# Pre-summed quarters of w2 made by accumulating transfers, the sampled tokens' output product placed inside an MLP product, a norm shift on another engine

## Chip, cores and metric

One core of a Trainium2 chip runs the whole program. The metric is the device time in microseconds from launch to end. The kernel before took 3325.08 us as the median of three runs (3316.52 to 3332.91). Everything is float32 on the outside. On TensorE each float32 product is made of three passes over a high and a low part of the operands, which are split by ScalarE (high part) and VectorE (low part).

## The reference, cut to what matters

One layer of a decoder: a joint input projection, a causal attention with forget gates (FoX) and a matrix memory (mLSTM) over 2048 prompt tokens, the same for 64 sampled tokens against a paged cache of 8192 positions per sequence, an output projection, and an MLP, with a layer norm after each.

```python
def _block_out(x, fox_h, m_h, og, mlstm_norm_w, w_o, ln1_g, ln1_b, w1, w2, ln2_g, ln2_b):
    ...
    mix = jnp.concatenate([fox_h, mn.astype(x.dtype)], axis=-1) @ w_o
    x1 = _layer_norm(DN_ALPHA * x + mix, ln1_g, ln1_b)
    hid = jnp.square(jax.nn.relu(x1 @ w1))
    return _layer_norm(DN_ALPHA * x1 + hid @ w2, ln2_g, ln2_b)
```

## The kernel before

The work runs in four stages on one core. Stage A (up to about 920 us) projects the inputs and runs the matrix memory. Stage B is the prompt's attention: 64 units, one for each head `h` (0 to 7) and group `g` (0 to 7) of 256 queries. Stage O multiplies the mixed heads by `w_o` and makes the first layer norm. Stage C is the MLP in four blocks of 512 tokens (`ci` 0 to 3); the fourth block also holds the 64 sampled tokens, as tile 16.

**The attention of the sampled tokens** is a generator of 294 steps that runs beside all of this. `tick(us)` adds modelled microseconds of TensorE work to a counter and takes one step of the generator for each `PACE` of them; `PACE_C` holds in stages O and C. A step of even number multiplies one gathered pair of cache pages; step `n` handles pair `(n - 38) / 2`, so the last of 128 pairs falls to step 292. Step 293 ends the last sequence, and then the result is written to DRAM (`dmix`). Seventy-eight steps and the gathers behind them are done when stage O begins. A call of `unit` in stage O is worth 5.1 modelled microseconds, a half of `hidden` 5.12, each of the 14 half products of `output` 1.28.

**The MLP** of a block goes over 16 slices of 256 hidden columns. `hidden(p, half)` makes one slice `hq` from `w1`, in two halves `f` = 0, 1 of 128 columns, and `output(p)` multiplies two slices by `w2` in seven products instead of eight (a Strassen-like scheme over 2 by 2 quarters). Four of the seven need sums of quarters of `w2`: b11+b12, b12+b22, b22+b11+b12 and b21+b22+b11+b12. They do not depend on the tokens, so they are made once, in stage B, by `w2_sums(p)` for `p` = 0 to 7, and kept in DRAM as `dw2`. One call loads the four quarters (512 KB each) through SyncE's queue into `wr` buffers, of which there are five, adds them in place on GpSimd in a chain of four additions (L1089), and stores each sum through GpSimd's queue (L1090). It is called at every sixth unit from unit 8 to unit 50.

**In stage B**, GpSimd also adds the causal mask to a row of forget values for each 128 queries (`nd`, L938, three buffers). VectorE's masked maximum of the diagonal block (L956) needs `nd`, and everything behind it on VectorE waits for it. VectorE also makes the low parts of queries and keys (`ql`, `ks`, L157, two SBUF inputs), and TensorE's scores (L945, L946) wait for these. ScalarE makes the exponentials (L973).

**The sampled tokens' end.** When the attention of the sampled tokens is through, `sampled()` reads `dmix` for them, multiplies it by `w_o` (eight pieces of weights, each split by ScalarE and VectorE), makes the first layer norm and stores it to `dx1`. The fourth block's last tile is read from there and transposed by TensorE (`px`, L1135) before that block can begin. In the third block (`ci` = 2) this is traced after `output(6)`, then `hidden(7, 1)`, then the rest of the attention's steps, then `sampled()`, then `output(7)`, which also transposes the next block's tiles.

**Second layer norms** of blocks 0 to 2 are carried out one by one in the next block's `hidden` calls (`later`): statistics on VectorE, power on GpSimd (L174), scale on ScalarE (L176), gain on VectorE (L177), shift on GpSimd (L178). The fourth block has a quicker form, `norm_quick`, which the change does not touch.

**The order of instructions** on an engine is chosen when the program is built: from the trace order, by a simulated timeline, so an instruction that is ready in that simulation can stand ahead of one traced earlier. `issue_after(ins)` keeps the instructions of its block behind `ins` on `ins`'s engine. At run time each engine takes its instructions in order.

Of the kernel before, what the change touches and what calls it, by code (L numbers as in the profile page):

```python
# [19 lines left out]

PACE_A = 5.6
PACE_B = float('inf')
PACE_C = 5
PACE_M = 2.3
D = 1024
S = 2048
# [26 lines left out]
def body(ctx, tc, I, O, stages):  # L53
# [811 lines left out]
    def phase_b():  # L865
# [172 lines left out]
        for n in range(len(units) + LA):  # L1038
            if 10 <= n < 16 and acc[1] is not None:
                attend()  # L1040
            if n % 6 == 2 and 8 <= n < 56:
                w2_sums(n // 6 - 1)
            if n == 60:
                wo.extend(half_wo(0, q) for q in range(4))
            if n < len(units):
                h, g = units[n]
                sc[n] = scores(Z[h], g)
                if h == 0 and g % 2 == 0 and g < 6:
                    keys(Z[0], g // 2 + 1)
                if h < 7:  # L1050
                    if g == 3:
                        Z[h + 1] = head(h + 1)
                        forget_values(Z[h + 1], 0, S)
                    if g >= 4:
                        keys(Z[h + 1], g - 4)
                if n + 1 < len(units):
                    queries(Z[units[n + 1][0]], units[n + 1][1])
            if n >= LA:
                h, g = units[n - LA]
                values(Z[h], g, sc.pop(n - LA))  # L1060
# [19 lines left out]

        return pcw.tile([128, 1024], F32, name="xr", bufs=2)[:n]

    def w2_sums(p):

        b11, b12, b21, b22 = (raw() for _ in range(4))
        for q, b in enumerate((b11, b12, b21, b22)):
            SY.dma_start(b, I["w2"][p, q])
        for q, (a, b) in enumerate(((b11, b12), (b12, b22), (b22, b11), (b21, b22))):
            G.tensor_tensor(a, a, b, op=OP.add)  # L1089
            G.dma_start(dw2[p, q], a)  # L1090

    def half_wo(hf, q):

# [46 lines left out]
    def phase_o(halves):  # L1140
        C["py"] = es_c.enter_context(tc.tile_pool(name="py", bufs=1, side="right", reuse_waits="tile"))
        C["pc"] = pc = es_c.enter_context(tc.tile_pool(name="pc", bufs=1, reuse_waits="tile"))
        es, es_b, es_x = ExitStack(), ExitStack(), ExitStack()
        po_ = es.enter_context(tc.tile_pool(name="po", bufs=1, reuse_waits="tile"))
        pob = es_b.enter_context(tc.tile_pool(name="pob", bufs=1, side="right", reuse_waits="tile"))
        ppo = es.enter_context(tc.tile_pool(name="ppo", bufs=1, space=PSUM, reuse_waits="tile"))

        def mix(t, eng):
            mr = landing().rearrange("p (k c) -> p k c", k=8)
            SY.dma_start(mr, dmv[:, :, t * 128:(t + 1) * 128])  # L1150
            mh = po_.tile([128, 8, 128], F32R, name="mh", bufs=2)
            ml = po_.tile([128, 8, 128], F32R, name="ml", bufs=2)
            split_hi(mh, mr)
            split_lo(ml, mr, mh, eng)
            return mh, ml

        vx["more"] = lambda: pob.tile([128, 1024], F32, name="vx", bufs=2)
        wh, wl = [[], []], [[], []]

        def weights(hf):  # L1160
            for q in range(4):
                r = halves.pop(0) if halves else half_wo(hf, q)
                if hf == 0:
                    h, l = piece(None, r)
                else:
                    h = pob.tile([128, 2, 512], F32R, name="woh", bufs=4)
                    l = pob.tile([128, 2, 512], F32R, name="wol", bufs=4)
                    split_hi(h, r)
                    split_lo(l, r, h)
                wh[hf] += [h[:, 0], h[:, 1]]  # L1170
                wl[hf] += [l[:, 0], l[:, 1]]

        m, xs = {}, {}

        def begin(t):
            xs[t] = row()
            SY.dma_start(xs[t], x_of(t))

        def unit(t, hf):
            s = slice(hf * 512, (hf + 1) * 512)  # L1180
            ps = ppo.tile([128, 512], F32, name="pw", bufs=4)
            for k in range(8):
                mm3(ps, m[t][0][:, k], m[t][1][:, k], wh[hf][k], wl[hf][k], k == 0, k == 7)
            V.scalar_tensor_tensor(xs[t][:, s], xs[t][:, s], ALPHA, ps, op0=OP.mult, op1=OP.add)
            tick(5.1)

        def end(t):
            layer_norm(xs[t], 128, *gb, pc, "1")
            SY.dma_start(dx1[t * 128:(t + 1) * 128], xs[t])

        m[0] = mix(0, None)
        weights(0)
        pad(pc, 192)
        m[1] = mix(1, None)
        begin(0)
        begin(1)
        unit(0, 0)
        weights(1)
        unit(1, 0)
        gb = [bcast(I[f"ln1_{x}"], 0, D, f"{x}1", pcw, tag="wr", bufs=5) for x in "gb"]  # L1200
        unit(0, 1)
        m[2] = mix(2, G)
        end(0)
        unit(1, 1)
        end(1)
        for t in range(2, 14):
            if t == 13:
                vx["more"] = None
            m[t + 1] = mix(t + 1, G)
            begin(t)  # L1210
            unit(t, 0)
            unit(t, 1)
            end(t)

        m[15] = mix(15, G)
        begin(14)
        begin(15)
        nx = [x1_load(0), x1_load(1)]
        unit(14, 1)
        take_back()  # L1220
        unit(15, 1)
        es_b.close()
        C["px"] = es_c.enter_context(tc.tile_pool(name="px", bufs=1, side="right", reuse_waits="tile"))
        ppx = es_x.enter_context(tc.tile_pool(name="ppx", bufs=1, space=PSUM, side="right", reuse_waits="tile"))
        px_of = lambda: ppx.tile([128, 4, 128], F32, name="px", bufs=2)
        x1_turn(0, 0, nx[0], px_of)
        nx.append(x1_load(2))
        unit(14, 0)
        x1_turn(1, 1, nx[1], px_of)
        nx.append(x1_load(3))  # L1230
        end(14)
        unit(15, 0)
        x1_turn(2, 2, nx[2], px_of)
        x1_turn(3, 3, nx[3], px_of)
        C["w1"] = w1_pieces(0)
        end(15)
        es_x.close()
        es.close()


    def phase_c():
# [41 lines left out]
        for ci, blk in enumerate(CB):  # L1283
# [3 lines left out]
            pieces = [(0, 512)] if W == 512 else [(0, 288), (288, 576)]  # L1287

            def hidden(p, half, between=None):
                w1p = C.pop("w1", None) or w1_pieces(half * 8 + p)  # L1290
                hq = H[p, half] = ph.tile([128, 2, 576], F32, name="hq", bufs=3)
                for f in range(2):
                    for (a, b) in pieces:
                        ps = ppc.tile([128, 512], F32, name="ph", tag="ph", bufs=2)[:, :b - a]
                        for k in range(8):
                            wh, wl = (x[:, k % 4, f * 128:(f + 1) * 128] for x in w1p[k // 4])
                            mm3(ps, wh, wl, xh[:, k, a:b], xl[:, k, a:b], k == 0, k == 7)
                        A.activation(hq[:, f, a:b], ps, AF.Relu)
                        A.activation(hq[:, f, a:b], hq[:, f, a:b], AF.Square)
                        tick((b - a) * 0.01)  # L1300
                    if f == 0 and between:
                        between()
                    if later:
                        later.pop(0)()
# [120 lines left out]

            def normed(t, y, gb):
                def go():
                    layer_norm(y, 128, *gb, pc, "2")
                    SY.dma_start(y_out(t), y)
                return go  # L1430

# [9 lines left out]
            for p in range(8):  # L1441
                pre = []
                if p < 7:
                    hidden(p + 1, 0, lambda: pre.append(ahead(p, 1, 5)))
                else:
                    pre.append(ahead(p, 1))
                if p == 6:
                    vx["more"] = None
                output(p, pre[0], begun if p == 7 and ci < 3 else None)
                if p == 7 and ci < 3:  # L1450
                    vx["more"] = landing
                    C["w1"] = w1_pieces(0)
                    C["gb"] = vecs(2)
                    later = [normed(t, ys[t], C["gb"]) for t in blk]
                if p == 6 and ci < 3:
                    take_back()
                    begun = [x1_load(t) for t in CB[ci + 1][:2]]
                if p < 7:
                    hidden(p + 1, 1)
                if p == 6 and ci == 2:  # L1460
                    while acc[1] is not None:
                        tick(100.0)
                    sampled()
        es.close()

    wo = []
# [430 lines left out]
```

## Time and profile before

| | |
|---|---|
| median of three runs | 3325.08 us (3316.52 to 3332.91) |
| the profiled execution | 3329.77 us, span 3328.0 us |
| granted TensorE clock, mean | 0.975 |
| TensorE busy | 3161.2 us, 95% |
| VectorE, ScalarE, GpSimd busy | 64%, 45%, 30% |
| HBM | 220 GB/s over the span |

In the views of the profile, PE is TensorE, DVE VectorE, ACT ScalarE, POOL GpSimd, SP SyncE; SPq, ACTq and POOLq are the sequencers that issue transfers. A row of a group names the line of the kernel, engine and operation, what is written from what (`out<-in`), the shape and the count, then the busy time and the mean of one in ns, and after the second bar the idle time of the engine just ahead of these instructions with what ended it. A row of windows gives the busy time of each engine in a stretch with the number of its instructions, then the granted clock (1.00 is full), the share of time in which the transfer engines were busy, and GB/s.

### The profile page before, as it was taken

The page shows a single profiled execution, that of the slowest core. Times are in us where ns is not written, and L with a number is a line of the kernel's source. Part 1 is how long each engine was busy: PE and PEld are TensorE (multiplying, and loading weights), DVE is VectorE, ACT ScalarE, POOL GpSimd, SP SyncE. Part 2 cuts the span into 40 slices and gives each one's busy share as a digit, 9 for nine tenths or more (in the row PEclk, how much of TensorE's full clock was granted, in tenths as well). Part 3 has the DMA queues.
Part 4 walks back from the last instruction along what each step waited for, and adds up shares of the span by engine and source line. Part 5 has one row for each costly group of instructions (what it writes and reads, how often), then busy time and mean ns, then how long its engine had stood idle before and what let it go on. Part 6 is the DMA issues. An engine that isn't in the chain of part 4 may idle for free.

```text
span 3328.0 us, 58130 instructions
## 1 busy us (share of the span) xinstructions
PE 3161.2 (95%) x21681; PEld 2575.1 (77%) x21681; DVE 2128.3 (64%) x5067; ACT 1505.5 (45%) x2966; POOL 986.0 (30%) x989
## 2 busy tenths in 40 slices
PE   8999999988969999999899999999999999799997
PEld 8998998887846666677677777677777777698895
DVE  6957565455378887644465667666577666756658
ACT  4333343333357788622244444353454444444442
POOL 0031242322346622276433224323244211110000
PEclk9999999998989999999999999999999999899998
DMA  5575766756687732387788877878789666544333
GB/s 184 156 220 186 231 221 220 259 201 225 197 254 247 244 103 61 113 309 247 276 301 285 289 276 268 333 250 314 283 287 341 237 214 211 181 155 127 114 108 98
DMA packets 339698, 734.37 MB, mean 221 GB/s; under 512 B 63640, under 2 KB 177688, under 8 KB 338520
## 3 DMA queue, kind: packets, MB, share of 16 engines
q1 hardware_dynamic: 257464, 433.49, 40.9%
q0 software_dynamic: 78912, 287.34, 23.2%
q10 hardware_dynamic: 3040, 9.83, 0.8%
q8 instruction: 171, 2.80, 0.3%
q14 instruction: 111, 0.91, 0.1%
HBM read 660.93 MB, written 69.60 MB: 220 GB/s over the span
## 4 chain that ended last, share of the span: by engine, by line
PE 41%; DMA 5%; issue 4%; DVE 2%; POOL 1%; ACT 0%; DVEq 0%; POOLq 0%; SPq 0%; ACTq 0%
PE ph L162 7%; PE ph L163 7%; PE ph L164 7%; PE py L162 5%; PE py L164 5%; PE py L163 5%; DMA vt<-cache_v,idxV 3%; PE sO L1753 2%; PE sQ L1641 2%; DMA xr<-cache_v,idxV 1%; DVE wl L157 1%; PE sT L1710 1%; DVE y L1316 1%; PE pw L163 0%; PE pw L164 0%
## 5 line engine op out<-in xcount | busy, mean ns | idle before, releaser
L157 DVE TENSOR_TENSOR wl<-wr,wh 128x1024 fp32r<-128x1024 f32 x364 | 451.6, 1243 | 377.8 <-ACT wh L154 377.3
L154 ACT ACTIVATE wh<-wr 128x1024 fp32r<-128x1024 f32 x364 | 382.9, 1054 | 352.9 <-PE ph L163 159.2
L1618 POOL DMA_INDIRECT kT<-cache_k,idxK x256 | 269.8, 1054 | 634.6 <-PE sQ L1641 572.9
L162 PE MATMUL ph<-x1h,wh 128*128 128x512 f32 (+1 forms) x1280 | 456.7, 357 | 0.5 <-DVE x1l L157 0.5
L163 PE MATMUL ph<-x1l,wh 128*128 128x512 f32 (+1 forms) x1280 | 454.0, 355 | 0.0
L164 PE MATMUL ph<-x1h,wl 128*128 128x512 f32 (+1 forms) x1280 | 451.7, 354 | 0.0
L162 PE MATMUL py<-wh,hh 128*128 128x512 f32 x896 | 356.0, 399 | 1.7 <-ACT hh L154 0.8
L163 PE MATMUL py<-wl,hh 128*128 128x512 f32 x896 | 352.1, 393 | 0.5 <-DVE wl L157 0.5
L164 PE MATMUL py<-wh,hl 128*128 128x512 f32 x896 | 350.0, 392 | 1.6 <-DVE hl L157 1.6
L1316 DVE TENSOR_TENSOR y<-y,py 128x512 f32<-128x512 f32 x416 | 280.8, 681 | 75.1 <-PE py L164 71.0
L162 PE MATMUL pm<-xh,whi 128*128 128x256 f32 (+1 forms) x1024 | 301.4, 294 | 0.1
L163 PE MATMUL pm<-xl,whi 128*128 128x256 f32 (+1 forms) x1024 | 296.8, 290 | 0.0
L164 PE MATMUL pm<-xh,wlo 128*128 128x256 f32 (+1 forms) x1024 | 295.9, 289 | 0.0
L162 PEld LDWEIGHTS ph<-x1h,wh 128*128 128x128 f32 x1280 | 241.7, 189 | 40.2 <-issue 7.0
L163 PEld LDWEIGHTS ph<-x1l,wh 128*128 128x128 f32 x1280 | 241.7, 189 | 33.4 <-issue 2.9
L164 PEld LDWEIGHTS ph<-x1h,wl 128*128 128x128 f32 x1280 | 241.4, 189 | 33.5 <-issue 2.9
L1729 POOL DMA_INDIRECT vt<-cache_v,idxV x164 | 171.1, 1043 | 301.6 <-PE sO L1753 228.8
L162 PE MATMUL pm<-whi,xh 128*128 128x256 f32 (+2 forms) x816 | 238.7, 293 | 8.2 <-ACT whi L154 8.2
L163 PE MATMUL pm<-wlo,xh 128*128 128x256 f32 (+2 forms) x816 | 234.2, 287 | 0.6 <-DVE wlo L157 0.6
L164 PE MATMUL pm<-whi,xl 128*128 128x256 f32 (+2 forms) x816 | 233.8, 287 | 0.0
L973 ACT ACTIVATE S<-S,mx 128x512 f32<-128x512 f32 (+2 forms) x320 | 207.7, 652 | 37.3 <-DVE mx L959 34.7
L162 PEld LDWEIGHTS py<-wh,hh 128*128 128x128 f32 x896 | 168.1, 188 | 52.5 <-issue 10.4
(370 smaller groups left out, 6934.9 us busy)
## 6 DMA issues: line engine op xcount, KB each, us to landing
wr<-w SPq DMA_DIRECT2D x256, 512.0 KB
wr<-dw SPq DMA_DIRECT2D x128, 512.0 KB
wra<-w_in SPq DMA_DIRECT2D x104, 512.0 KB
Rb<-dR SPq DMA_DIRECT2D x128, 128.0 KB
dw<-wr POOLq DMA_DIRECT2D x32, 512.0 KB, 4.2
xn<-xp_t SPq DMA_DIRECT2D x16, 512.0 KB
kn<-k_prompt SPq DMA_DIRECT2D x64, 128.0 KB
qn<-dq SPq DMA_DIRECT2D x128, 64.0 KB
```

The lines of the kernel that those rows point to most:

```text
L154: last["ACT"] = A.activation(dst, src, AF.Copy, scale=scale)
L157: r = (eng or V).tensor_tensor(dst, src, hi.bitcast(F32), op=OP.subtract)
L162: T.matmul(ps, wh, xh, start=first, stop=False, skip_group_check=shared)
L163: T.matmul(ps, wh, xl, start=False, stop=False, skip_group_check=shared)
L164: last["PE"] = T.matmul(ps, wl, xh, start=False, stop=stop, skip_group_check=shared)
L973: last["ACT"] = A.activation(sp[:, :w], sp[:, :w], AF.Exp, bias=mx[:, 7:8], accum_out=lp[:, k:k + 1])
L1316: V.tensor_tensor(y, y, ps, op=op)
L1618: G.indirect_dma_start(out=piece(n), out_offset=None, in_=ck, in_offset=IO(ap=idxK[:, b, j // 2, j % 2:j % 2 + 1], axis=0))
L1641: r = T.matmul(pq[h4 * 32:h4 * 32 + 32, hg].rearrange("p (k c) -> p k c", k=2), z["qb"][:, hd], kv, start=(db == 0), stop=(db == 1), skip_ ...
L1710: T.transpose(p[:, f], z["U"][u][:, hg, f].rearrange("p k t -> p (k t)"), ident)
L1729: G.indirect_dma_start(out=vt.rearrange("p f c -> p (f c)"), out_offset=None, in_=cv, in_offset=IO(ap=idxV[:, b, (kt % 4) * 4 + kt // 4, f ...
L1753: after_ = T.matmul(po[r:r + 32], z["PT"][:, hg, 2 * f + g, pg].rearrange("p h q -> p (h q)"), vts[f][:, g, hg * 256:(hg + 1) * 256], star ...
```

## The change

Five edits. (1) `w2_sums` becomes `w2_sum`, called 34 times, at every one and a half units from unit 10 to unit 59. Two quarters (b11 and b22) are loaded for each `p`, through ScalarE's queue; the others are added to them by transfers that accumulate into SBUF, issued by GpSimd; the sums are stored by GpSimd as before. The 32 additions on GpSimd are gone. (2) In the third block the remaining attention steps come ahead of `hidden(7, 1)`, and `sampled` is traced between that product's two halves instead of after it; `PACE_C` goes from 5 to 4.93. (3) The shift of the second layer norm of blocks 0 to 2 goes from GpSimd to VectorE. (4) At the end of stage O, tile 2 is transposed before the norm of tile 14 and the first-half product of tile 15 instead of after them. (5) The low parts of `w1` are kept behind the split that was traced last on VectorE.

```diff
-PACE_C = 5
+PACE_C = 4.93
...
-            if n % 6 == 2 and 8 <= n < 56:
-                w2_sums(n // 6 - 1)
+            while len(w2_done) < 34 and n >= 10 + len(w2_done) * 3 // 2:
+                w2_sum()
...
-    def w2_sums(p):
-
-        b11, b12, b21, b22 = (raw() for _ in range(4))
-        for q, b in enumerate((b11, b12, b21, b22)):
-            SY.dma_start(b, I["w2"][p, q])
-        for q, (a, b) in enumerate(((b11, b12), (b12, b22), (b22, b11), (b21, b22))):
-            G.tensor_tensor(a, a, b, op=OP.add)
-            G.dma_start(dw2[p, q], a)
+    w2_done, w2_q = [], {}
+
+    def w2_sum():
+
+        k = len(w2_done)
+        w2_done.append(k)
+
+        def load(p):
+            for q in (0, 3):
+                w2_q[p, q] = raw()
+                with tc.issue_after(last["ACT"].ins):
+                    A.dma_start(w2_q[p, q], I["w2"][p, q])
+
+        def add(p, a, q):
+            G.dma_start(w2_q[p, a], I["w2"][p, q], accum_op=OP.add)
+
+        def store(p, a, j):
+            G.dma_start(dw2[p, j], w2_q[p, a])
+
+        p, j = divmod(k, 4)
+        if k == 0:
+            load(0)
+        if j == 0:
+            if p:
+                store(p - 1, 0, 2)
+                add(p - 1, 0, 2)
+            if p < 8:
+                add(p, 0, 1)
+        elif j == 1:
+            if p:
+                store(p - 1, 0, 3)
+            if p < 8:
+                store(p, 0, 0)
+                add(p, 3, 1)
+        elif j == 2:
+            store(p, 3, 1)
+            add(p, 0, 3)
+        elif p < 7:
+            load(p + 1)
...
         end(14)
         unit(15, 0)
-        x1_turn(2, 2, nx[2], px_of)
...
             def hidden(p, half, between=None):
-                w1p = C.pop("w1", None) or w1_pieces(half * 8 + p)
+                with tc.issue_after(last["DVE"].ins):
+                    w1p = C.pop("w1", None) or w1_pieces(half * 8 + p)
...
-                    layer_norm(y, 128, *gb, pc, "2")
+                    layer_norm(y, 128, *gb, pc, "2", V)
...
-                if p < 7:
-                    hidden(p + 1, 1)
                 if p == 6 and ci == 2:
                     while acc[1] is not None:
                         tick(100.0)
-                    sampled()
+                if p < 7:
+                    hidden(p + 1, 1, sampled if p == 6 and ci == 2 else None)
```

(The line that transposes tile 2 now stands ahead of `end(14)`.)

More of the change, by code (lines that the diff above doesn't have):

```diff
@@ L1230, in phase_o @@
         nx.append(x1_load(3))
+        x1_turn(2, 2, nx[2], px_of)
         end(14)
         unit(15, 0)
-        x1_turn(2, 2, nx[2], px_of)
         x1_turn(3, 3, nx[3], px_of)
```

## The prediction

> **What bounds the kernel now.** I read the page first (busy shares, then the slices of PE and of the granted clock), then the windows of stage B, then the groups and waits of the stretches that stood out.
>
> ```profile
> span 3328.0 us, 58130 instructions
> PE 3161.2 (95%) x21681; PEld 2575.1 (77%) x21681; DVE 2128.3 (64%) x5067; ACT 1505.5 (45%) x2966; POOL 986.0 (30%) x989
> PE   8999999988969999999899999999999999799997
> PEclk9999999998989999999999999999999999899998
> ```
>
> TensorE sets the time: it is busy 3161 of 3328 us, so no edit can bring more than the 167 us of idle time and what the clock loses beside it. The change touches three of the stretches where that time lies: the first part of stage B (slices 12 to 14), the turn from stage O to C (slice 20), and the end of the third MLP block (slices 34 and 35). In stage B the sums of w2 fall between 958 and 1157 us; the stretch behind them has the same work without them.
>
> ```profile
> 958.00:1157.00 199.00, 178.62 (x1145) 125.56 (x1146) 171.26 (x560) 148.28 (x417) 136.08 (x132) 0.92 0.75 245
> 1157.00:1346.00 189.00, 186.97 (x1290) 129.28 (x1287) 150.78 (x615) 161.49 (x458) 44.97 (x75) 1.00 0.29 87
> ```
>
> With the sums TensorE does 1145 matmuls in 199 us, without them 1290 in 189 us (6.83 a us), at which rate the 1145 take 168 us. So the sums cost about **31 us**: 20.4 us of idle TensorE and the rest in the clock (0.92) and in slower rows. What ends the idle time:
>
> ```profile
> L945 PE MATMUL pS<-ks,qh 128*128 128x512 f32 (+2 forms) x131 | 59.0, 452 | 14.0 <-DVE mx L956 8.5 <-DVE mx L952 4.6 <-DVE mx L959 0.7
> L946 PE MATMUL pS<-ks,ql 128*128 128x512 f32 (+2 forms) x132 | 51.1, 390 | 4.1 <-DVE ql L157 4.1
> ...
> L945 PE MATMUL pS<-ks,qh 128*128 128x512 f32 (+2 forms) x142 | 59.8, 424 | 0.6 <-DVE mx L959 0.2
> L946 PE MATMUL pS<-ks,ql 128*128 128x512 f32 (+2 forms) x142 | 51.5, 367 | 0.0
> ...
> L157 DVE TENSOR_TENSOR ql<-qn,qh 128x256 fp32r<-128x256 f32 x27 | 32.4, 1200 | 0.1
> L157 DVE TENSOR_TENSOR ks<-kn,ks 64x512 fp32r<-64x512 f32 x15 | 20.3, 1362 | 0.4
> ...
> L157 DVE TENSOR_TENSOR ql<-qn,qh 128x256 fp32r<-128x256 f32 x29 | 13.7, 474 | 1.3 <-ACT qh L154 1.3
> L157 DVE TENSOR_TENSOR ks<-kn,ks 64x512 fp32r<-64x512 f32 x12 | 8.1, 691 | 1.1 <-ACT ks L154 0.8
> ```
>
> (First pair of each kind: 958 to 1157; second pair: 1157 to 1346.) VectorE is late, and the rows that grew are those with two operands in SBUF: a `ql` takes 1200 ns instead of 474, a `ks` 1362 instead of 691. That is 27 x 0.73 + 15 x 0.67 = 30 us of VectorE, the size of the loss. TensorE's waits go over from 18.1 us to 0.6 us.
>
> **The change part by part. The sums.** What leaves GpSimd and what stays:
>
> ```profile
> L1089 POOL TENSOR_TENSOR wr<-wr 128x1024 f32<-128x1024 f32 x32 | 76.3, 2385 | 17.7 <-DMA wr<-w 13.0 <-issue 4.3
> ...
> L1090 POOL DMA_DIRECT2D dw<-wr x32: 538/568/606, 959.5 to 1157.1; - x32
> ...
> DMA to landing us min/median/max: 2.9/4.2/6.2
> ...
> L938 POOL TENSOR_TENSOR nd<-nl,dmask 128x128 f32<-128x128 f32 x59 | 29.4, 502 | 122.0 <-DVE mx L956 79.7 <-DVE ls L974 37.3 <-DVE mx L959 4.9
> ...
> L1378 ACTq DMA_DIRECT2D y<-dx x17: 326/411/912, 1656.1 to 2932.4; - x17
> kT<-cache_k,idxK POOLq DMA_INDIRECT x256, 9.0
> ...
> DMA to landing us min/median/max: 4.0/9.4/15.0
> ```
>
> (The last row is the landing of the gathers into `xr`, the slowest in this trace.) The 32 additions, 76.3 us, go. GpSimd then issues 32 stores and 32 accumulating transfers, 64 x 0.568 = 36 us over units 10 to 59, beside 24% of other work (44.97 of 189 us): it has room. ScalarE issues 16 loads, 16 x 0.41 = 6.6 us, at 85% busy (161.49 of 189): TensorE covers it, and without that cover it costs 6.6. SyncE loses 32 loads. The transfers thin out: 64 in 199 us become 80 in 50 units.
>
> What is new is the waiting on GpSimd. A unit lasts 6.75 us:
>
> ```profile
> 958.00:1157.00 199.00, 59.15 (x447) 28.53 (x449) 10.18 (x25) 9.07 (x25) 0.92 0.75 245
> 1157.00:1346.00 189.00, 68.01 (x524) 32.58 (x520) 11.03 (x27) 9.87 (x28) 1.00 0.29 87
> ```
>
> (Windows of the instructions on `po`: TensorE, weight loads, VectorE, ScalarE; ScalarE empties `po` once a unit, 28 times in the 189 us.) Four calls serve one `p`, so they have 6 units, 40.5 us. In them the first buffer goes through three additions in series and one store that an addition must await: 3 L + 4.2 us, where L is the landing of an accumulating transfer. Nothing here shows L. From below it is the plain store's 4.2 us, from above the 15.0 us of the slowest gather. It reads its target too, so I take twice the plain one, about 8 us, near the gathers' 9.0. Then 3 x 8 + 4.2 = 28 us fit into 40.5. Behind a waiting GpSimd stand `nd` and the scaling of finished heads; `nd` has three buffers, 1.5 units or 10 us ahead, and in the quiet stretch GpSimd already idles 79.7 us for VectorE to free one. A wait up to 10 us is hidden by that; beyond it VectorE's L956 is late, then the scores.
>
> The Trainium skill (Collectives: The Full Stack, "The bandwidth ceiling: the fold count and why AG ≠ RS ≠ AR") says that a reducing transfer is slower not by the addition but by its second source read, which halves its rate. By it L is at most twice 4.2 us, and the sum keeps its value; no run here shows it yet.
>
> I let 5 us of the 31 stay (ScalarE's issues, the first load and addition in one call, transfers beside heads that were quiet): **-26 us**, between -38 (the same rate taken by the 447 and 524 products of `po` alone would give 38) and, with L within 12 us, -8.
>
> **The end of the third block.**
>
> ```profile
> 2838.18 0.39 PE L162 MATMUL ph<-x1h,wh 128*128 128x512 f32 x1
> ...
> 2840.67 0.40 PE L164 MATMUL ph<-x1h,wl 128*128 128x512 f32 x1
> ...
> 2842.23 1.07 PE L1753 MATMUL sO<-vt,PTs 128*32 128x256 f32 x16 [0.72 <-DMA vt<-cache_v,idxV]
> ...
> 2849.71 1.94 PE L1135 MATMUL px<-ident,xr 128*128 128x128 f32 x8 [3.20 <-DMA xr<-dx]
> ...
> 2855.39 0.48 PE L162 MATMUL py<-wh,mhs 128*64 128x256 f32 x1 [1.20 <-ACT mhs L154]
> ...
> 2901.57 1.08 PE L1135 MATMUL px<-ident,xr 64*128 64x64 f32 x8 [11.33 <-DMA xr<-dx]
> ...
> 2846.91 0.43 SPq L1841 DMA_DIRECT2D dmix<-mixs  x1
> 2851.76 0.37 SPq L1255 DMA_DIRECT2D mxs<-dmix  x1
> ...
> 2891.92 0.48 SPq L1271 DMA_DIRECT2D dx<-y  x1
> 2896.72 0.48 SPq L1123 DMA_DIRECT2D xr<-dx  x1
> ...
> L162 PE MATMUL ph<-x1h,wh 128*128 128x512 f32 x16 | 6.4, 397 | 0.0
> ...
> 2842.00:2903.00 61.00, 41.93 (x238) 33.41 (x238) 49.75 (x77) 27.39 (x37) 4.94 (x3) 0.83 0.60 192
> ```
>
> From the last value product (2842.23) a chain runs to the transposes of tile 16 (2901.57): out to `dmix`, back to `mxs`, the sampled product from 2855.39, its norm, out to `dx1`, back to `xr`. In those 61 us TensorE is idle 19.1 us, 11.33 of them in one wait, with the clock at 0.83. `hidden(7, 1)` stands just before the chain: 48 matmuls, one each 0.226 us (12 from 2838.18 to 2840.67, 11 steps), 10.9 us. The change moves it inside: the first half, 5.4 us, beside the trip through `dmix`; the second behind the sampled product, beside the norm. For this the attention must end 10.9 us earlier. Modelled time up to that point: 32 x 5.1 in stage O, 2 x 307.2 for two blocks (32 halves x 5.12 and 112 x 1.28), and 15 x 10.24 + 98 x 1.28 in the third, 1056.6. At 5 that is 211 steps, at 4.93 it is 214; with the 78 done before, step 289 becomes 292, the last value product. So it ends inside `output(6)`. TensorE's work stays, 10.9 us of it now fill idle time: **-11 us**, with bounds 0 (the chain grows as much) and -19 (all idle time goes, clock included).
>
> **The rest.** Tile 2's transposes ahead of a product of 5.1 us; the norm's shift; the order of `w1`'s low parts:
>
> ```profile
> 1627.38 1.97 PE L1135 MATMUL px<-ident,xr 128*128 128x128 f32 x8 [3.87 <-DVE x1l L157]
> ...
> L177 DVE TENSOR_TENSOR y<-y,g 128x1024 f32<-128x1024 f32 (+1 forms) x29 | 36.7, 1264 | 15.0 <-ACT y L176 14.8
> L178 POOL TENSOR_TENSOR y<-y,b 128x1024 f32<-128x1024 f32 (+1 forms) x29 | 74.0, 2551 | 65.0 <-DVE y L177 38.2 <-DVE ln_rs L173 26.6
> ...
> 2050.00:2100.00 50.00, 50.00 (x303) 38.12 (x301) 37.74 (x58) 25.85 (x37) 25.17 (x17) 1.00 0.77 273
> ```
>
> The 3.87 us wait is for transposed tiles at the end of the stage; starting one earlier takes half of it, **-2 us** (bounds -4 and +4, if its load is not there yet). Twelve shifts cost VectorE 12 x 1.26 = 15 us and free GpSimd of 12 x 2.55 = 31 us and their waits. They lie where TensorE is busy 50.00 of 50 us and VectorE 37.74, so 0 (uncovered, 15 us; if gathers behind the shifts come sooner, -3). The order of the low parts and the denser steps: 0, bounds -2 and +5.
>
> **Sum** against the profiled execution's 3329.8 us (span 3328.0 and 1.8 around it): -26 - 11 - 2 = -39, 3291 us. The median of the runs is 4.7 us lower: **3286 us**.
>
> **Rivals.** *The third block gives nothing* (13%). The norm chain runs on a VectorE that is 49.75 of 61 us busy, and the sampled pieces share four buffers with the two of `w1` that are held through the product. If it grows by 11 us, 3325 - 28 = 3297 us. Against it: TensorE's second half of `hidden` needs neither.
>
> *The contention stays* (10%): VectorE's rows grow not from GpSimd's additions but from the transfers (share 0.75 against 0.29), or the accumulating issues hold VectorE as the additions did. Then only 13 us are left, 3312 us. For it: both differ between the two windows. Against it: only the rows with two SBUF operands grew, and transfers do not choose rows. The Trainium skill (SBUF — State Buffer, "Summary: rules for kernel authors") says that transfers issued by GpSimd starve beside VectorE's fast modes; the 32 issues of 538 to 606 ns beside an 86% busy VectorE do not show it.
>
> *Slower: GpSimd waits for the accumulating transfers* (11%). If L is over (40.5 - 4.2) / 3 = 12.1 us, each `p` lasts 3 L + 4.2 us and `nd` falls behind after its 10 us are used. At L = 15.0 that is 8 x (49.2 - 40.5) = 70 us more, 3286 + 70 = 3356 us; the gain is used up at L = 13.7. For it: 15.0 us stands in the trace. Against it: that was behind many gathers, and stage B's plain stores land within 6.2.
>
> **How the numbers follow.** My forecast has 66%. 0.5% is 16.6 us, about what a measurement of this kernel can tell from no change, so faster means below 3308. That holds for nearly all of the first case and the first rival, and a little of the second: 0.79. Same: the rest of the second, 0.09. Slower: 0.12. The range: low, all bounds of the three gains partly together (-38 - 19 - 4 = -61, hardly all at once), 3264 us; high, past the second rival's 3312 with the 8 us by which the runs spread, 3320 us. It leaves out the slower case.
>
> **What would show it.** Right: `ql` near 0.47 us through all of stage B, the clock at 1.00 from unit 10 on, the transposes' 11.33 us wait near 6. Wrong: waits of GpSimd's stores and additions over 10 us with `nd` late behind them, accumulating transfers landing after 12 us, or a stage B as long as before.

## The result, and the profile after

The changed kernel takes 3320.03 us (median of 20 runs, 3305.77 to 3328.09) against 3323.49 us before (20 runs, 3313.71 to 3332.91): a ratio of 0.9983, 95% interval 0.9971 to 0.9994. That is 3.5 us gained, not 39. The profiled execution took 3327.42 us, its span 3325.7 us.

The head of the page, and the windows of stage B cut as they were before (columns: TensorE, weight loads, VectorE, ScalarE, GpSimd, granted clock, DMA share, GB/s):

```profile
span 3325.7 us, 58093 instructions
PE 3155.1 (95%) x21681; PEld 2571.7 (77%) x21681; DVE 2106.5 (63%) x5079; ACT 1504.9 (45%) x2966; POOL 928.8 (28%) x977
PE   8999999998978989999999999999999999799997
PEclk9999999998988999999999999999999999999998
```

```profile
958.00:1157.00 199.00, 185.20 (x1237) 129.07 (x1236) 154.23 (x598) 158.61 (x446) 69.93 (x103) 0.96 0.72 192
1157.00:1346.00 189.00, 175.96 (x1182) 122.85 (x1180) 142.84 (x571) 149.78 (x421) 66.97 (x102) 0.96 0.74 197
```

The loss has been spread, not removed. Before, the first window held 1145 products and the second 1290; now they hold 1237 and 1182, 2419 in all against 2435, and the clock is 0.96 in both. Stage B, from its first `pS` to its last `po`, lasted 469.9 us before and 472.3 us now. Groups of the same two windows:

```profile
L945 PE MATMUL pS<-ks,qh 128*128 128x512 f32 (+2 forms) x141 | 61.2, 436 | 10.7 <-DVE mx L956 9.5 <-DVE mx L952 0.8 <-DVE mx L959 0.2
...
L157 DVE TENSOR_TENSOR ql<-qn,qh 128x256 fp32r<-128x256 f32 x29 | 16.0, 551 | 0.1
L956 DVE CUSTOM_DVE_ANT_0 S<-pS,nd 128x128 f32<-128x128 f32 x54 | 15.4, 285 | 11.6 <-POOL nd L938 11.0 <-PE pS L946 0.5
...
L945 PE MATMUL pS<-ks,qh 128*128 128x512 f32 (+2 forms) x133 | 57.5, 435 | 12.4 <-DVE mx L959 7.9 <-DVE mx L956 4.5
...
L956 DVE CUSTOM_DVE_ANT_0 S<-pS,nd 128x128 f32<-128x128 f32 x55 | 15.7, 285 | 15.3 <-POOL nd L938 14.8 <-PE pS L946 0.4
L157 DVE TENSOR_TENSOR ql<-qn,qh 128x256 fp32r<-128x256 f32 x27 | 14.7, 547 | 0.7 <-ACT qh L154 0.6
```

(First three: 958 to 1157; last three: 1157 to 1346.) A `ql` takes 551 and 547 ns where it took 1200 and 474: VectorE's slow rows are gone, but for some 0.08 us each. Its L956, however, the masked end of a score row, now stands idle 25.8 us for `nd` from GpSimd, and TensorE's scores wait behind it as they did for the slow rows. The waits of stage B, 958 to 1400 (us in total, times, longest):

```profile
POOL dw L1100 <- DMA wr<-w: 93.2, 27, 6.3
...
POOL wr L1097 <- DMA dw<-wr: 35.3, 14, 6.4
...
DVE S L956 <- POOL nd L938: 25.8, 5, 8.4
```

The same in the groups of GpSimd:

```profile
L1097 POOL DMA_DIRECT2D wr<-w x32 | 29.5, 939 | 59.6 <-DMA dw<-wr 35.3 <-DMA wr<-w 20.5 <-DMA drl<-lt 3.3
L1100 POOL DMA_DIRECT2D dw<-wr x32 | 18.9, 590 | 99.3 <-DMA wr<-w 93.2 <-DMA rl<-drl 5.8 <-issue 0.2
```

No single wait for one of these transfers is over 6.4 us, yet five times `nd` is late. GpSimd's own line shows how (start, duration, idle before and its releaser):

```profile
1036.78 0.59 POOL L1100 DMA_DIRECT2D dw<-wr  x1 [0.58 <-DMA wr<-w]
1040.21 0.90 POOL L1097 DMA_DIRECT2D wr<-w  x1 [2.85 <-DMA dw<-wr]
1040.80 0.80 POOL L938 TENSOR_TENSOR nd<-nl,dmask 128x128 f32<-128x128 f32 x1
1046.70 0.58 POOL L1100 DMA_DIRECT2D dw<-wr  x1 [5.10 <-DMA wr<-w]
1053.36 0.88 POOL L1097 DMA_DIRECT2D wr<-w  x1 [6.08 <-DMA dw<-wr]
1053.96 0.76 POOL L938 TENSOR_TENSOR nd<-nl,dmask 128x128 f32<-128x128 f32 x1
1059.68 0.58 POOL L1100 DMA_DIRECT2D dw<-wr  x1 [4.96 <-DMA wr<-w]
1060.27 1.89 POOL L938 TENSOR_TENSOR nd<-nl,dmask 128x128 f32<-128x128 f32 x4
```

Store, addition, store, addition, store: each waits for the landing of the one before it, and in the 23.5 us from 1036.78 to 1060.27 only two `nd` get through, where a unit of 6.75 us wants two. Then four come at once, which shows that their buffers had been free: VectorE was waiting for them. By the prediction's reckoning three buffers of `nd` carry 10 us; the five waits add up to 19.6.

The accumulating transfers in the same stretch, and what they are set against, the stores:

```profile
L1097 POOL DMA_DIRECT2D wr<-w x32: 877/902/1550, 1000.0 to 1327.3; - x32
...
DMA to landing us min/median/max: 5.4/6.1/9.5
...
L1100 POOL DMA_DIRECT2D dw<-wr x32: 549/583/897, 1006.1 to 1333.7; - x32
...
DMA to landing us min/median/max: 2.9/4.2/9.4
```

An accumulating transfer of 512 KB lands 6.1 us after its issue (a plain store 4.2) and occupies GpSimd 902 ns for the issue (a store 583).

At the end of the third block the last value product of the attention started at 2834.8 us and the last transpose of tile 16 at 2900.1, 65.3 us later (before: 2843.5 to 2902.3, 58.9 us). The window around it:

```profile
2834.00:2901.00 67.00, 49.34 (x289) 40.64 (x281) 54.98 (x89) 31.93 (x42) 8.11 (x4) 0.92 0.66 205
```

The timeline there: the last product of `hidden(7, 1)` and the first sampled one on TensorE, its last long wait, and the sampled norm on VectorE.

```profile
2846.59 0.39 PE L164 MATMUL ph<-x1h,wl 128*128 128x512 f32 x1
...
2847.17 0.36 PE L162 MATMUL py<-wh,mhs 128*64 128x256 f32 x1
...
2899.32 1.08 PE L1166 MATMUL px<-ident,xr 64*128 64x64 f32 x8 [12.74 <-DMA xr<-dx]
...
2862.59 0.41 DVE L1300 SCALAR_TENSOR_TENSOR y<-y,py 64x256 f32<-64x256 f32 x1
2866.14 0.68 DVE L169 BATCH_NORM_STATS2 ln_st<-y 64x6 f32<-64x512 f32 x1
2871.39 0.20 DVE L171 BATCH_NORM_AGGREGATE ln_mv<-ln_st 64x2 f32<-64x12 f32 x1
2876.19 0.14 DVE L173 TENSOR_SCALAR ln_rs<-ln_mv 64x1 f32<-64x1 f32 x1
...
2881.52 0.20 DVE L175 TENSOR_SCALAR ln_rs<-ln_mv,ln_rs 64x1 f32<-64x1 f32 x1
...
2886.30 1.21 DVE L177 TENSOR_TENSOR y<-y,g 64x1024 f32<-64x1024 f32 x1
```

The wait at the last transposes was to fall from 11.33 to near 6 us; it is 12.74. Both halves of `hidden(7, 1)` ran ahead of the sampled product on TensorE (the last of its products at 2846.6, the first sampled one at 2847.2), so they filled the trip through `dmix` and nothing was left for the norm. From the last addition to the sampled rows (L1300) to their gain (L177) the norm is five short instructions, each 3.6 to 5.3 us behind the one before, among the splits and additions of `output(7)` on a VectorE that is 54.98 of 67 us busy. That stretch lasts 23.7 us; before it was 16.9, so the 6.4 us by which the chain has grown lie there. Its two ends before:

```profile
2869.85 0.41 DVE L1269 SCALAR_TENSOR_TENSOR y<-y,py 64x256 f32<-64x256 f32 x1
...
2886.71 1.22 DVE L177 TENSOR_TENSOR y<-y,g 64x1024 f32<-64x1024 f32 x1
```

### The profile page after: what moved, and what is told of

The parts are those of the page before. It is cut to its first block, busy times and chain, and to the rows that moved or that the text cites. A ratio compares the mean times of both kernels' runs of the same rounds, so it can differ in the third digit from the quotient of the medians.

```text
span 3325.7 us, 58093 instructions
## 1 busy us (share of the span) xinstructions
PE 3155.1 (95%) x21681; PEld 2571.7 (77%) x21681; DVE 2106.5 (63%) x5079; ACT 1504.9 (45%) x2966; POOL 928.8 (28%) x977
## 4 chain that ended last, share of the span: by engine, by line
PE 45%; DMA 4%; DVE 2%; issue 1%; POOL 1%; ACT 0%; DVEq 0%; POOLq 0%; ACTq 0%; SPq 0%
PE ph L162 8%; PE ph L163 7%; PE ph L164 7%; PE py L162 5%; PE py L164 5%; PE py L163 5%; PE sO L1784 3%; DMA vt<-cache_v,idxV 2%; PE sQ L1672 2%; DMA kT<-cache_k,idxK 1%; PE sT L1741 1%; DVE wl L157 1%; DVE y L1348 1%; DMA xr<-cache_v,idxV 0%; PE pw L163 0%
## 5 line engine op out<-in xcount | busy, mean ns | idle before, releaser
L1760 POOL DMA_INDIRECT vt<-cache_v,idxV x164 | 178.9, 1091 | 342.0 <-PE sO L1784 276.8
```

What stands on the lines that cost most here:

```text
L1760: G.indirect_dma_start(out=vt.rearrange("p f c -> p (f c)"), out_offset=None, in_=cv, in_offset=IO(ap=idxV[:, b, (kt % 4) * 4 + kt // 4, f ...
```

## The experiments

Theory 1: the additions did cost about 30 us, and the change gives them back because dependent transfers stand back to back in GpSimd's line, with `nd` behind them. Rivals: the transfers' traffic or their issues hold the stage; or the sums gained and the other four edits lost. "Stage B" is the time from the first `pS` to the last `po` in the profiled execution; ratios are to the kernel before, on the same chip.

**Edit 1 alone.** The kernel before with the new `w2_sum` and its call.

> The kernel before with edit 1 alone (the sums by accumulating transfers). Theory 1, GpSimd's waits in line give back what the additions cost: stage B stays within 10 us of the 470 us before, VectorE's L956 waits 20 us or more for nd, the whole is 0.997 to 1.002 of before. Rival, the sums gain their 26 us and the other four edits lose them again: stage B 440 to 450 us, the whole 0.992 of before (3298 us).

3325.0 us, ratio 0.9996 (0.9983 to 1.0008), stage B 465.0 us. Groups on VectorE, 958 to 1400:

```profile
L157 DVE TENSOR_TENSOR ql<-qn,qh 128x256 fp32r<-128x256 f32 x59 | 33.1, 562 | 1.1 <-ACT qh L154 0.9
...
L956 DVE CUSTOM_DVE_ANT_0 S<-pS,nd 128x128 f32<-128x128 f32 x120 | 34.2, 285 | 21.0 <-POOL nd L938 19.0 <-PE pS L946 1.9
```

The edit takes the slow rows away, brings in the wait for `nd` (19.0 us, a little under the 20 expected), and is worth nothing as a whole.

**Edits 2 to 5 alone.** The kernel after with the old `w2_sums` and its call.

> The kernel after with the old sums (edits 2 to 5 alone). Theory 1: these edits bring only the 4 to 6 us of the third block, 0.998 to 0.999 of before (3317 to 3320 us). Rival, they lose what edit 1 gains: 1.006 of before or more (3343 us).

3319.92 us, 0.9979 (0.9967 to 0.9992), stage B 470.3 us. The other four edits lose nothing; as far as the intervals tell, they are the whole 0.2% of the change. That rival falls.

**More buffers of `nd`.**

```diff
-                nd = pb.tile([128, 128], F32, name="nd", bufs=3)
+                nd = pb.tile([128, 128], F32, name="nd", bufs=8)
```

> The kernel after with eight buffers of nd instead of three, so that nd can be made 20 us or more ahead. Theory 1 (waits of 17 us stacked up ahead of nd): L956's 25.8 us of waiting for nd fall below 5, stage B loses 15 to 30 us, the whole is 0.989 to 0.994 of before. Rivals, the traffic of the transfers or the 0.90 us issues themselves hold the stage: as after, 0.998 of before, stage B 470 us.

3305.91 us, 0.9942 (0.9928 to 0.9956), stage B 453.2 us. Its group, 958 to 1400:

```profile
L956 DVE CUSTOM_DVE_ANT_0 S<-pS,nd 128x128 f32<-128x128 f32 x119 | 33.8, 284 | 2.7 <-PE pS L946 1.6 <-POOL nd L938 0.9
```

The wait for `nd` goes from 25.8 to 0.9 us with the same transfers, and the stage loses 19 us. GpSimd's transfers keep their order and their waits (161 us idle before them, against 159); only the place of `nd` moved. Five more `nd` run ahead of each of the first 16 transfers. Behind those the order is the old one to within one `nd`, and there GpSimd only waits less for VectorE to free a buffer (its idle time before `nd` falls from 92.3 to 59.4 us). So the late `nd` was what gave most of the gain back. Not all of it: in the next run, without the additions, the stage is 11 us shorter still.

**No additions.** The kernel before without them, loads and stores kept.

```diff
-            G.tensor_tensor(a, a, b, op=OP.add)
```

> The kernel before without GpSimd's 32 additions; the quarters are loaded and stored as they are, so the same traffic remains and the sums of w2 are left out. If the additions are the whole of the 31 us: ql at 0.47 us in the sums' stretch, stage B 440 to 447 us, the whole 0.991 to 0.993 of before. If the transfers' traffic slows VectorE: ql over 1 us still, 0.999 to 1.000 of before.

3295.01 us, 0.9915 (0.9899 to 0.9932), stage B 442.1 us. Its window of the sums, and the group of its `ql` there:

```profile
958.00:1157.00 199.00, 194.20 (x1336) 136.14 (x1334) 163.07 (x648) 170.47 (x480) 64.10 (x107) 1.00 0.80 269
```

```profile
L157 DVE TENSOR_TENSOR ql<-qn,qh 128x256 fp32r<-128x256 f32 x32 | 15.8, 493 | 0.6 <-ACT qh L154 0.4
```

With a DMA share of 0.80 the clock is 1.00, TensorE does 1336 products instead of 1145, and a `ql` takes 493 ns. The slow rows came from the additions, not from the traffic, and they cost 28 us: the prediction's 31 us was the right prize.

**GpSimd's order written out.** The kernel after, `nd` with three buffers, `w2_sum` replaced by single steps paced by the units' work; each DMA of GpSimd is held behind the `nd` of its score tile, and the next `nd` behind it.

```diff
-                G.tensor_tensor(nd, nl[:, qt * 128:n], dmask, op=OP.add)
+                with ExitStack() as es_n:
+                    if "POOL" in last:
+                        es_n.enter_context(tc.issue_after(last["POOL"].ins))
+                    last["POOL"] = G.tensor_tensor(nd, nl[:, qt * 128:n], dmask, op=OP.add)
+                if z["h"] * 8 + g >= 10:
+                    w2_pace(z["h"], g)
...
+        w2_at[1] += (g + 1) / 2
+        while w2_at[0] < 62 and w2_at[1] > 3.6 * w2_at[0]:
+            w2_step(w2_at[0])
+            w2_at[0] += 1
...
+        if j == 0 and now:
+            add(p, 0, 1)
+        if j == 1 and old:
+            add(p - 1, 0, 2)
+        if j == 1 and now:
+            add(p, 3, 1)
+        if j == 2 and now:
+            store(p, 0, 0)
+        if j == 3 and old:
+            store(p - 1, 0, 3)
+        if j == 3 and now:
+            store(p, 3, 1)
+        if j == 4 and now:
+            add(p, 0, 3)
+        if j == 5 and p < 7:
+            load(p + 1)
+        if j == 6 and now:
+            store(p, 0, 2)
```

> The kernel after, nd with its three buffers, but GpSimd's order written out: one step of the sums at a time, each behind the nd of its score tile, and no step behind the one it depends on until some 10 us (two steps) later. Theory 1 (what costs is that dependent transfers stand back to back in GpSimd's line): the waits of L956 for nd fall from 25.8 us to under 5, the stores' and additions' waits to under 40 us together, stage B 440 to 453 us, the whole 0.990 to 0.994 of before. Rival, the transfers themselves (share 0.8 to 0.9 of the DMA engines, 0.90 us an issue) cost the rest: no better than the eight buffers of nd, 453 us or more.

3307.2 us, 0.9949 (0.9934 to 0.9963), stage B 459.2 us. Its groups on VectorE and GpSimd, 958 to 1400:

```profile
L961 DVE CUSTOM_DVE_ANT_0 S<-pS,nd 128x128 f32<-128x128 f32 x117 | 33.3, 285 | 2.7 <-PE pS L951 2.6
...
L1105 POOL DMA_DIRECT2D wr<-w x32 | 29.0, 960 | 15.2 <-DMA dw<-wr 7.1 <-DMA wr<-w 6.0 <-PE pS L951 1.9
L1109 POOL DMA_DIRECT2D dw<-wr x32 | 18.3, 573 | 24.1 <-DMA wr<-w 22.6 <-DMA rl<-drl 1.1 <-issue 0.3
```

The same 64 transfers with the same three buffers, in another order and at another pace: GpSimd's idle time before them falls from 158.9 us (59.6 before L1097 and 99.3 before L1100 in the changed kernel) to 39.3, L956 no longer waits for `nd`, and the time falls by about as much as with eight buffers. Theory 1 holds from a second side. The stage is longer than was expected of it, though, by 6 us, and 453 us or more was to be the sign of the rival that the transfers themselves cost the rest. What holds the 17 us over the kernel without additions (442.1) is open. One place where they show is ScalarE, which now issues the quarters' loads: TensorE's transposes wait 12.2 us in all for its copies (`PT`) here, 1.0 us without the additions. That these loads are the reason is not shown.

**Plain loads in the place of the accumulating ones.**

```diff
-            G.dma_start(w2_q[p, a], I["w2"][p, q], accum_op=OP.add)
+            G.dma_start(w2_q[p, a], I["w2"][p, q])
```

> The kernel after with plain loads over the first quarters in place of the accumulating ones, in the same places and order; the sums of w2 are left out. If the accumulation itself is what is slow: landings fall from 6.1 to 3 to 4.2 us, the issue from 0.90 to 0.58 us, the wait of L956 for nd from 25.8 to under 10 us and stage B to 450 us. If it is the chain of dependent transfers in GpSimd's line, whatever they do: nd's wait stays at 15 us or more, stage B over 460 us.

3313.82 us (one run), stage B 454.2 us. The transfers copy where they should add, so this kernel leaves the sums out; its instructions on GpSimd stand in the changed kernel's order. When a load has landed is not in this trace. Its groups, 958 to 1400:

```profile
L956 DVE CUSTOM_DVE_ANT_0 S<-pS,nd 128x128 f32<-128x128 f32 x119 | 33.9, 285 | 10.3 <-POOL nd L938 8.0 <-PE pS L946 2.1
...
L1100 POOL DMA_DIRECT2D dw<-wr x32 | 18.2, 568 | 63.5 <-DMA wr<-w 63.2 <-issue 0.2
L1097 POOL DMA_DIRECT2D wr<-w x32 | 18.0, 562 | 55.6 <-DMA dw<-wr 31.5 <-DMA wr<-w 13.4 <-DMA drl<-lt 6.3
```

The expectation set the two causes against each other, and the answer is that both are needed. With plain loads the issue falls to 562 ns, the stores wait 63 us instead of 93, and the wait for `nd` falls to 8.0 us. So the chain in GpSimd's line costs because its links are slow: at this length of link it just passes the three buffers, with shorter ones it mostly does not.

**The sampled product one output earlier.**

```diff
-PACE_C = 4.93
+PACE_C = 4.74
...
-                if p == 6 and ci == 2:
+                if p == 5 and ci == 2:
...
-                    hidden(p + 1, 1, sampled if p == 6 and ci == 2 else None)
+                    hidden(p + 1, 1, sampled if p == 5 and ci == 2 else None)
```

> The kernel after with the attention's end and the sampled product one output earlier (inside hidden(6, 1), PACE_C 4.74), so that output(6) and hidden(7, 0) stand behind the sampled norm on TensorE. If the third block lost its 11 us because no product was left behind the sampled product while its norm waits in VectorE's line: the 12.7 us wait at the last transposes vanishes, the third block is 10 to 15 us shorter, 0.994 to 0.996 of before. If the norm's chain costs TensorE nothing or the denser steps cost as much: 0.998 as after.

3311.14 us, 0.9959 (0.9946 to 0.9973). Its window from the last value product on:

```profile
2793.00:2854.00 61.00, 60.34 (x314) 50.65 (x311) 48.32 (x71) 31.37 (x39) 2.95 (x2) 1.00 0.68 207
```

In the 61 us in which TensorE was idle 19.1 us before, it is idle 0.7 us, at a clock of 1.00, and the wait at the last transposes is gone. That is 8 to 9 us on top of the changed kernel; the two intervals just touch (0.9973 and 0.9971). The denser steps of the attention did not take it back.

**The second half of `hidden(7, 1)` behind the sampled product.**

```diff
+                        es_p = ExitStack()
+                        if f == 1 and between is sampled:
+                            es_p.enter_context(tc.issue_after(last["PE"].ins))
...
+                        es_p.close()
```

> The kernel after with the second half of hidden(7, 1) held behind the sampled product on TensorE, as the prediction had it. If the order of the halves was what failed: the wait for the last transposes falls from 12.7 to about 7 us, but the first gap (the trip through dmix) opens by as much, so the gain is under 4 us: 0.997 to 0.998 of before. If the second half was worth its 5.4 us by the norm: 0.996.

3312.91 us, 0.9971 (0.9957 to 0.9986). Its waits of TensorE from 2838 to 2876, the longest of each end:

```profile
2842.93 0.47 PE L162 MATMUL py<-wh,mhs 128*64 128x256 f32 x1 [4.83 <-ACT mhs L154]
...
2871.94 0.65 PE L1166 MATMUL px<-ident,xr 128*128 128x128 f32 x4 [2.95 <-DVE x1l L157]
```

The 12.74 us at tile 16 are gone altogether, and 4.83 us open before the sampled product. The chain goes from 65.3 to 62.7 us. The order of the halves matters in the way the prediction said, but it is worth 2.6 us of the chain, and the interval of the whole overlaps the changed kernel's: the two gaps share one product.

**Both together.** Eight `nd` buffers and the early sampled product.

> The kernel after with eight buffers of nd and the sampled product one output earlier. The two lie in different stages and should add: 0.994 less 0.003 to 0.004, 0.989 to 0.991 of before. If stage B's loss or the third block's comes back elsewhere: 0.993 or more.

3289.09 us, 0.9906 (0.9892 to 0.9921). The two add, as stages that do not touch each other should.

**The loads on SyncE.** Both together, with the 16 loads of the quarters issued by SyncE and held behind nothing.

```diff
-                with tc.issue_after(last["ACT"].ins):
-                    A.dma_start(w2_q[p, q], I["w2"][p, q])
+                SY.dma_start(w2_q[p, q], I["w2"][p, q])
```

> The kernel with eight nd buffers and the early sampled product (e8), with the 16 loads of w2's quarters issued by SyncE instead of ScalarE. If what is left over the 442 us of stage B without additions is ScalarE, held 2 to 4 us by a load in its line (PT copies late, then the transposes): stage B 443 to 449 us, 0.987 to 0.989 of before. If it is the accumulating transfers themselves: as e8, 0.9906, stage B 455 us.

3312.49 us, 0.9958 (0.9941 to 0.9975), stage B 466.7 us: worse, which neither theory had. Its windows and one wait (958 to 1127):

```profile
958.00:1010.00 52.00, 44.26 (x295) 31.20 (x293) 39.44 (x152) 39.83 (x114) 22.67 (x36) 0.99 1.06 297
...
1075.00:1127.00 52.00, 47.52 (x332) 34.29 (x330) 39.92 (x160) 41.57 (x119) 23.10 (x36) 0.98 1.02 300
...
1250.00:1352.00 102.00, 101.15 (x703) 70.78 (x703) 82.19 (x336) 86.52 (x247) 25.54 (x38) 1.00 0.19 57
```

```profile
ACT qh L154 <- DMA qn<-dq: 14.7, 6, 4.4
```

Without the hold the sums ran off to the front: the DMA share is about 1.0 up to 1127 us and 0.19 behind 1250. At that share the queries' own loads, which SyncE issues too, come late (14.7 us of waiting for `qn`). So the traffic, or its place in one line with the small loads, does cost at a share near 1; at 0.80, without the additions, it did not. The run tests the pace, not ScalarE.

**The written order with the loads on SyncE, and on ScalarE.** Both have eight `nd` buffers, the early sampled product and the paced single steps; they differ in the loads' engine.

> e9 with GpSimd's order written out besides (one step at a time, dependent steps 10 us apart). If eight nd buffers already hide every wait of GpSimd: the same as e9 within 0.001. If GpSimd's remaining waits still cost (the scaling of finished heads behind them): 2 to 6 us less than e9.

> e10 with the 16 loads back on ScalarE's line (each behind the last Exp), so that against e8 only GpSimd's order differs and against e10 only the loads' engine. If ScalarE's loads are what e10 took out: stage B 451 to 456 us, 0.9905 of before, as e8. If the written-out order is what e10 gained: stage B 445 to 449 us, 0.988 to 0.9895.

On SyncE 3293.19 us, 0.9889 (0.9864 to 0.9913), stage B 446.4 us; on ScalarE 3281.08 us, 0.9865 (0.9843 to 0.9886), stage B 455.4 us in a profiled execution that was the slowest of its six. The first is 19 us faster than the run before it, where 2 to 6 were expected. Its loads stand on SyncE as well, but paced (a DMA share of 0.83 between 958 and 1157 us), so SyncE's line alone was not what cost there.

Between the loads' engines the evidence is split. In the profiles stage B is 9 us shorter on SyncE, and TensorE's transposes wait 3.4 us for ScalarE's copies where they wait 9.3; but the intervals of the whole overlap, so no cost of ScalarE's loads is shown. The second, measured on another chip against its own runs of the kernel before, is 42 us faster than before, and its interval lies below that of the eight buffers with the early sampled product (0.9892 to 0.9921). Where in the kernel those last 8 us lie is open: its stage B is as long as in that version (455.4 us in both).

## Why the prediction was wrong

**The cost of the additions** was right: 31 us predicted, 28 us measured by leaving them out. **The rows with two SBUF operands** as their mark was right too: `ql` fell from 1.20 to 0.55 us (0.47 was forecast), and the rival of a contention that stays falls.

**The step that failed** is this one: "A wait up to 10 us is hidden by that". It took the waits one at a time, and none of them reached 10 us: the longest is 6.4. They come stacked. Each call issues two or three transfers, some of which need the one before, and the order on GpSimd's line put store, addition and store next to each other with a single `nd` between; five waits in a row reached 19.6 us. The sum that was made, 3 L + 4.2 us in 40.5, is a rate. It counts one store that an addition must await, where the code has two on the first buffer; with both, 3 x 6.1 + 2 x 4.2 = 26.7 us, and the sums still keep up. A rate says nothing of the longest run without an `nd`. The issues were mis-sized too, without harm to GpSimd's busy share (28%): 48 us (29.5 + 18.9) where 64 x 0.568 = 36 were reckoned. Because of the stacked waits the -26 us became 0 (edit 1 alone: 0.9996); the bound of -8 us at this landing had no working behind it. Of the prediction's signs of being wrong, a stage B as long as before came, and `nd` was late; but no wait was over 10 us, and no transfer landed after 12.

**The landing** was estimated at 8 us and measured at 6.1, 1.45 times the plain store's 4.2. The estimate drawn from the Trainium skill (Collectives: The Full Stack, "The bandwidth ceiling: the fold count and why AG ≠ RS ≠ AR"), at most twice the plain one, holds for the median here. The slower rival named the right mechanism, GpSimd waiting with `nd` behind it, and the wrong point from which it decides: 12.1 us of landing, where at 6.1 it already took back the whole gain. Its other half, slower than before, did not come.

**The end of the third block** was mis-sized. Edits 2 to 5 together give 7 us (0.9979). Of the 10.9 us of product moved in, the chain gave back 6.4 by growing from 58.9 to 65.3 us. The step that failed is "the second behind the sampled product, beside the norm": on TensorE it ran ahead of it. The rival that the block gives nothing had named where the chain would grow, in the norm on a busy VectorE (23.7 us against 16.9). Holding the half behind brought the wait down as written, but also opened the first gap; a whole output behind the sampled product closed both.

**Tile 2's transposes** were to give 2 us and gave none: the wait of 3.87 us for `x1l` stands unchanged behind the change.

```profile
1631.06 1.97 PE L1166 MATMUL px<-ident,xr 128*128 128x128 f32 x8 [3.87 <-DVE x1l L157]
```

The step that failed is "starting one earlier": from the first of these transposes to the last, TensorE's line holds the same instructions in the same order as before, each 3.7 us later. The edit changed where tile 2 is traced, but not the order that was built; why not is open.

**The rest at nothing** fits as far as it was seen: no computing engine waits for the twelve shifts (L178) on VectorE, and edits 2 to 5 as a whole are a gain. It was not tried edit by edit.

The range's top, 3320 us, just misses the median. With both failed steps mended (eight buffers, early sampled product) the kernel takes 3289 us, near the forecast of 3286, but that is in part luck: the gain is 31 us (0.9906) and not 39, of which the sums bring some 14 instead of 26, and the third block some 15 instead of 11.

## What to carry to other kernels

When work is moved from an engine's arithmetic to transfers that the engine issues, its waits can become the cost: write down the order in its line, add up the waits between two instructions that others need, and hold that sum against the buffers, not each wait and not the rate. Either give the needed instruction more buffers, or fix the order so that no transfer stands close behind the one that it depends on; here each was worth 0.3 to 0.4% over the changed kernel. A product that is to fill a gap must be long enough for every gap of the chain, and must be held where it is wanted, since the order in which it was traced does not hold it there.

## What the runs showed of the hardware

An accumulating transfer of 512 KB from HBM into SBUF, issued by GpSimd, landed in 6.1 us (5.4 to 9.5), and its issue took 0.90 us of GpSimd; a plain load's issue in the same place took 0.56. Beside these transfers a `ql` on VectorE took 0.55 us, against 0.47 in a quiet stretch and 1.20 beside GpSimd's additions. At a DMA share of 0.80 TensorE's granted clock was 1.00 and it did 1336 products in 199 us; at 1.0, with the big loads issued by the same engine, small loads came up to 4.4 us late.
